# A hybrid decoder step on one core: two right sides in one product, two heads in one bank, and steps emitted a little after they are ready

## The chip, the core and the metric

The kernel runs on one core of one Trainium2 chip. The metric is the device time of one execution in microseconds; an execution is also profiled, and the profile gives the times of single instructions. Engines are called as in the profile: PE (TensorE) with PEld for its weight loads, DVE (VectorE), ACT (ScalarE), POOL (GpSimd) and SP (SyncE, which issues most transfers).

## The reference

One layer of a decoder for 1024 prompt tokens and 8 sequences of 8 new tokens, 1024 features:

```
h = rms_norm(x) * (1 + scale) + shift          # scale, shift, gate from silu(c) @ w_ada
P = h @ w_in                                   # RWKV columns, pooling columns, gate columns
for each token t, head by head (8 heads of 64):    # the RWKV-7 state
    sa = S @ (-kk_t)
    S = S * w_t + outer(sa, kk_t * a_t) + outer(v_t, k_t)
    y_t = S @ r_t
merged = sigmoid(g_A) * (A @ w_br_rwkv) + sigmoid(g_B) * (B @ w_br_pool)
x = x + gate * (merged @ w_out)
x = x + gate2 * (square(relu(h2 @ w_ff1)) @ w_ff2)
```

A is y after a group norm, a bonus and an output gate; B is a causal multi-scale mean of the pooling columns. The prompt starts from a zero state, each sequence from its own. All is float32; outputs are the rows of x after a last norm and the new states.

## The kernel before, in words

Features lie on partitions, the 1088 tokens along the free axis. A large product is done in three passes of rounded high and low parts (mm3): a row of 128 output features takes three chunks of 362 or 364 tokens. These large products are the backlog of the first stage: 34 blocks of w_in, then 8 blocks of w_br for the pooling branch, 36 or 72 products each. The output stage follows with 8 blocks of w_br for the RWKV branch (or_job), whose first 27 products read the rows of the first three head pairs and whose 28th is the first to read the rows of the fourth; then come w_out and the two layers of the channel mixer.

Beside the backlog run the head pairs f = 0 to 3 (two heads of 64 features each on the two halves of the partitions, HB). For each, front makes decay, keys and values, scores and unit make the products of a chunk of 64 tokens in groups of eight chunks (u = 0, 1) and of the 64 sequence tokens (u = 2), inverse and level make z, the inverse of a triangular matrix per chunk, affine applies z (first) and folds the result into the chunk's matrices (second), chain carries the state S through 16 chunks, sample does the sequences, and post makes the rows of A. The state chain is serial: a step's two products (ra with S into pn, S with ra into py, line 1138 and 1141) read S, and DVE makes the next S from pn (line 1139). In the trace these are wc<-S,ra, wc<-ra,S and the DVE writes of S. A product of line 358 has the helper's line, so tiles tell them apart: w<-at,z and w<-uv,z are first's two products with z (lines 1086 and 1087), w<-ab,at is second's (1099), w<-hv,ra and w<-ra,hv are the sequences' products with their states (1179 and 1194), w<-wt,kct are the head sums in the last post (1247 and 1252).

PE runs its instructions in the order in which the program emits them. That order is planned while the program is built. Pace holds a planned time; the backlog yields after each three products, and generators for chains, heads and pools yield what they wait for. Need is such a wait: at() is the planned time at which tiles are ready and PSUM banks free, and the step is emitted when the planned time has passed it. Where PE is amid large products, a ready step is held back up to `wait` ns more, so that several small steps share a trip from large to small products; where PE is at small products it is emitted at once. need has wait=500, and the chain's steps have wait=LS[f], with LS = (1200, 1200, 1200, 400). The planned times of DVE, ACT and POOL come from Clocks, which places each operation by a formula. PSUM has four banks of tag mm, two of w and two of wc.

Two orders of the heads matter below: a front for f writes bk only when the first half of the chain f-1 is done, and unit 1 starts when its second half is done.

Of the kernel before, what the change touches and what calls it, by code (L numbers as in the profile page):

```python
# [13 lines left out]
ALU = mybir.AluOpType  # L14
# [199 lines left out]
class Need:  # L214


    def __init__(self, k, aps, banks, wait):
        self.k, self.aps, self.banks, self.wait = k, aps, banks, wait

    def at(self):  # L220
        return max([self.k.clocks.ready(*self.aps)] + [self.k.clocks.free(b, self.k.pb[b], self.banks.count(b)) for b in set(self.banks)])
# [100 lines left out]
class K:  # L322
# [55 lines left out]
    def need(self, *aps, banks=("w",), wait=500):  # L378
        return Need(self, aps, banks, wait)
# [529 lines left out]
    def unit(self, f, d, u):  # L909
# [11 lines left out]
        Q = dict(ab=tl("ab", [2, 128]), ak=tl("ak", [64], 1), uv=tl("uv", [2, 64]), ra=d["qs"][u]["ra"])  # L921
        d["qs"][u] = Q
        ra, ab, ak, uv = Q["ra"], Q["ab"], Q["ak"], Q["uv"]
        if prompt:
            Q["at"] = tl("at", [64])
            strict, incl = self.kc("strict"), self.kc("incl")
        else:
            strict, incl = self.kc("strict8"), self.kc("incl8")
        for a in range(0, C, 4):
# [43 lines left out]
        if prompt:  # L973
            nc.vector.tensor_copy(Q["at"], cut(pa))
# [7 lines left out]
        if prompt:  # L982
# [6 lines left out]
            for h, os in enumerate((HB[1], HB[0])):  # L989
                nc.scalar.activation(uv[os, :, h, :], cut(ps[os, :]), AF.Copy)  # L990
# [84 lines left out]
    def affine(self, f, d):  # L1075
# [4 lines left out]
        def first(u):  # L1080
            Q = d["qs"][u]
            uv, w = Q["uv"], Q["at"]
# [24 lines left out]
        for u in range(2):  # L1107
            Q = d["qs"][u]
            yield self.need(z, Q["at"], Q["uv"], banks=("w", "w"))
# [5 lines left out]
    def chain(self, f, d):  # L1115
# [4 lines left out]
        for u in range(2):  # L1120
# [9 lines left out]
            for i in range(8):  # L1130
# [12 lines left out]
                if i < 7:  # L1143
                    yield self.need(S, banks=(), wait=LS[f])
# [12 lines left out]
    def sample(self, f, d):  # L1157
# [11 lines left out]
        px = self.ps("w")  # L1169
# [982 lines left out]
```

## Time and profile before

| | |
|---|---|
| timed runs, us | 1657.31, 1648.69, 1647.8 (median 1648.69) |
| profiled execution, us | 1655.5, span 1653.4 |
| PE busy | 1578.5 us, 95% of the span |
| DVE, ACT, POOL busy | 66%, 41%, 8% |
| granted PE clock, mean | 0.98 |
| first head's products to the output stage | 85 to 794.5 us |
| output stage to the end | 794.5 to 1653.4 us |

A row of the timeline gives start, length, engine, line, operation with output tile and inputs, shape and count, and in brackets the idle time of the engine before it and what ended it. Each float32 product leaves two records, each of the large products (float32r) one. The granted clock is a share of full speed; busy time at a granted clock of 0.66 is longer than it would be at 1.00.

### The profile page before, as it was taken

The page shows a single profiled execution, that of the slowest core. Times are in us where ns is not written, and L with a number is a line of the kernel's source. Part 1 is how long each engine was busy: PE and PEld are TensorE (multiplying, and loading weights), DVE is VectorE, ACT ScalarE, POOL GpSimd, SP SyncE. Part 2 cuts the span into 40 slices and gives each one's busy share as a digit, 9 for nine tenths or more (in the row PEclk, how much of TensorE's full clock was granted, in tenths as well). Part 3 has the DMA queues.
Part 4 walks back from the last instruction along what each step waited for, and adds up shares of the span by engine and source line. Part 5 has one row for each costly group of instructions (what it writes and reads, how often), then busy time and mean ns, then how long its engine had stood idle before and what let it go on. Part 6 is the DMA issues. An engine that isn't in the chain of part 4 may idle for free.

```text
span 1653.4 us, 35059 instructions
## 1 busy us (share of the span) xinstructions
PE 1578.5 (95%) x14363; PEld 1476.4 (89%) x14363; DVE 1091.4 (66%) x1912; ACT 674.3 (41%) x1297; POOL 137.7 (8%) x200
## 2 busy tenths in 40 slices
PE   4999999998899999999999999999999999999997
PEld 2898778887788778989999999999999999999997
DVE  5585566755659384736453578999766786666775
ACT  4455354453244444623222365222333444434651
POOL 0110011000000000000430120000000041000000
PEclk9999998999799899999999999999999999999999
DMA  9232512242223422385696456666434997665663
GB/s 345 85 106 95 181 64 86 88 162 72 70 72 102 137 87 97 107 316 187 232 340 231 154 172 204 211 218 216 174 140 145 385 355 246 200 198 158 214 200 122
DMA packets 121857, 288.28 MB, mean 174 GB/s; under 512 B 21120, under 2 KB 26752, under 8 KB 121696
## 3 DMA queue, kind: packets, MB, share of 16 engines
q1 hardware_dynamic: 113312, 264.65, 46.5%
q10 hardware_dynamic: 8240, 20.95, 3.7%
q8 instruction: 113, 1.85, 0.5%
q14 instruction: 48, 0.39, 0.1%
q0 software_dynamic: 144, 0.44, 0.1%
HBM read 208.70 MB, written 77.28 MB: 173 GB/s over the span
## 4 chain that ended last, share of the span: by engine, by line
PE 66%; DVE 8%; DMA 4%; ACT 2%; issue 2%; SPq 0%; DVEq 0%; ACTq 0%
PE mm L358 44%; PE wc L358 11%; PE w L358 11%; DVE wt L187 2%; DMA hid<-in_w_ff 1%; DVE hx L187 1%; DMA mg<-in_w_ff 1%; DVE bk L187 1%; DVE wlo L187 1%; DVE hv L187 1%; DMA hid<-in_w_ada_mlp 1%; DMA wt<-d_x 1%; ACT L187 0%; ACT wt L187 0%; PE w L389 0%
## 5 line engine op out<-in xcount | busy, mean ns | idle before, releaser
L358 PE MATMUL mm<-hx,whi 128*128 128x362 f32 (+2 forms) x2944 | 689.9, 322 | 3.9 <-ACT px L187 2.5
L358 PEld LDWEIGHTS mm<-hx,whi 128*128 128x128 f32 x2944 | 497.7, 190 | 29.4 <-issue 12.8
L358 PE MATMUL mm<-hx,wlo 128*128 128x362 f32 (+2 forms) x1472 | 463.9, 315 | 4.7 <-issue 2.4
L358 PEld LDWEIGHTS mm<-hx,wlo 128*128 128x128 f32 x1472 | 280.0, 190 | 2.8 <-DVE wlo L187 2.8
L358 PE MATMUL mm<-mg,whi 128*128 128x272 f32 (+2 forms) x1312 | 249.4, 289 | 0.1
L358 PEld LDWEIGHTS mm<-mg,whi 128*128 128x128 f32 x1312 | 205.3, 188 | 4.5 <-issue 2.5
L358 PE MATMUL mm<-mg,wlo 128*128 128x272 f32 (+2 forms) x656 | 188.5, 287 | 0.0
L358 PE MATMUL wc<-hx,whi 128*128 128x272 f32 x896 | 170.4, 287 | 0.0
L358 PEld LDWEIGHTS wc<-hx,whi 128*128 128x128 f32 x896 | 140.3, 188 | 0.0
L187 ACT ACTIVATE whi<-hid 128x512 fp32r<-128x512 f32 x128 | 80.4, 630 | 143.7 <-PE mm L358 59.4
L358 PE MATMUL wc<-hx,wlo 128*128 128x272 f32 x448 | 128.8, 287 | 0.8 <-DVE wlo L187 0.8
L358 PEld LDWEIGHTS mm<-mg,wlo 128*128 128x128 f32 x656 | 123.5, 188 | 0.0
L187 DVE TENSOR_TENSOR wlo<-hid,whi 128x512 fp32r<-128x512 f32 x128 | 87.9, 687 | 47.8 <-ACT whi L187 47.0
L187 DVE TENSOR_TENSOR wlo<-wraw,whi 128x512 fp32r<-128x512 f32 x84 | 60.8, 725 | 72.8 <-ACT whi L187 70.0
L187 ACT ACTIVATE whi<-wraw 128x512 fp32r<-128x512 f32 x100 | 62.6, 628 | 107.1 <-PE mm L358 59.3
L358 PE MATMUL w<-hx,whi 128*128 128x272 f32 (+1 forms) x480 | 97.6, 297 | 0.0
L358 PEld LDWEIGHTS wc<-hx,wlo 128*128 128x128 f32 x448 | 84.2, 188 | 1.0 <-DVE wlo L187 1.0
L187 POOL TENSOR_TENSOR hx<-hx,rs 128x64 f32<-128x64 f32 x24 | 35.2, 1465 | 569.0 <-DMA mg<-in_w_ff 379.7
L358 PEld LDWEIGHTS w<-hx,whi 128*128 128x128 f32 x480 | 77.5, 189 | 0.2 <-issue 0.2
L358 PEld LDWEIGHTS mm<-mg,hx 128*128 128x128 f32 x576 | 72.9, 188 | 5.0 <-issue 5.0
L358 PE MATMUL mm<-mg,hx 128*128 128x272 f32 (+2 forms) x576 | 75.5, 290 | 0.0
L358 PE MATMUL w<-hx,wlo 128*128 128x272 f32 (+1 forms) x240 | 71.1, 296 | 1.0 <-DVE wlo L187 1.0
(268 smaller groups left out, 2376.1 us busy)
## 6 DMA issues: line engine op xcount, KB each, us to landing
t<-d_t SPq DMA_DIRECT2D x56, 544.0 KB, 4.9
hid<-in_w_ff SPq DMA_DIRECT2D x110, 256.0 KB, 3.8
d_t<-hx SPq DMA_DIRECT2D x102, 272.0 KB, 2.2
hid<-in_w_ff SPq DMA_DIRECT2D x42, 512.0 KB, 3.9
wraw<-in_w_in SPq DMA_DIRECT2D x68, 256.0 KB, 2.9
mg<-in_w_ff SPq DMA_DIRECT2D x58, 256.0 KB, 5.4
hid<-in_w_ada_mlp SPq DMA_DIRECT2D x24, 512.0 KB, 5.9
d_th<-px SPq DMA_DIRECT2D x22, 544.0 KB, 3.1
```

Source lines behind the costliest of these rows:

```text
L187: return f(*a, **kw)
L358: return self.nc.tensor.matmul(out, lhsT, rhs, **kw)
```

## The change

The first two products with z have the same left side, z of a chunk. Before, their right sides lay in two tiles (at and the far half of uv); now at has room for both side by side, and first makes one product of 128 columns, four chunks to a bank. The strict product ak of the prompt's units shares at's second half, and the product of ak and uv is put there in one ACT operation instead of two. first empties each bank with three operations of four chunks, six in all, instead of three of eight.

In sample the two heads' products with the states are put in one bank and emitted one behind the other (before, a bank each, with a wait between), one DVE operation masks both, and the 16 products of 8 columns alternate between the heads.

In the planner, need's wait goes from 500 to 1000 and a new `spare` is added to the time at which tiles are ready (not to that of the banks): 300 ns, and 700 for the chain's steps; LS becomes (2500, 2500, 2500, 300).

```diff
@@ class Need
-    def __init__(self, k, aps, banks, wait):
-        self.k, self.aps, self.banks, self.wait = k, aps, banks, wait
+    def __init__(self, k, aps, banks, wait, spare):
+        self.k, self.aps, self.banks, self.wait, self.spare = k, aps, banks, wait, spare
     def at(self):
-        return max([self.k.clocks.ready(*self.aps)] + [self.k.clocks.free(b, self.k.pb[b], self.banks.count(b)) for b in set(self.banks)])
+        return max([self.k.clocks.ready(*self.aps) + self.spare] + [self.k.clocks.free(b, self.k.pb[b], self.banks.count(b)) for b in set(self.banks)])
-    def need(self, *aps, banks=("w",), wait=500):
+    def need(self, *aps, banks=("w",), wait=1000, spare=300):
@@ unit
         if prompt:
-            Q["at"] = tl("at", [64])
+            at = Q["at"] = tl("at", [2, 64])
+            ak = at[:, :, 1, :]
         else:
+            ak = Q["ak"] = tl("ak", [64])
-            nc.vector.tensor_copy(Q["at"], cut(pa))
+            nc.vector.tensor_copy(at[:, :, 0, :], cut(pa))
-            for h, os in enumerate((HB[1], HB[0])):
-                nc.scalar.activation(uv[os, :, h, :], cut(ps[os, :]), AF.Copy)
+            nc.scalar.activation(at[:, :, 1, :], cut(ps), AF.Copy)
@@ affine, first
-            pw, pu = self.ps("w"), self.ps("w")
+            pss = [self.ps("w") for _ in range(2)]
             for i in range(8):
-                for h, os in enumerate((HB[1], HB[0])):
-                    self.mm(pw[os, i * 64:(i + 1) * 64], z[os, 8 * u + i, :], w[os, i, :], start=True, stop=True)
-                    self.mm(pu[os, i * 64:(i + 1) * 64], z[os, 8 * u + i, :], uv[os, i, h, :], start=True, stop=True)
-            nc.scalar.activation(w, cut(pw), AF.Copy)
-            nc.vector.tensor_copy(uv[HB[1], :, 0, :], cut(pu[HB[1], :]))
-            nc.scalar.activation(uv[HB[0], :, 1, :], cut(pu[HB[0], :]), AF.Copy)
+                for os in HB[::-1]:
+                    self.mm(pss[i // 4][os, i % 4 * 128:(i % 4 + 1) * 128], z[os, 8 * u + i, :], at[os, i, :, :].rearrange("p s j -> p (s j)"),
+                            start=True, stop=True)
+            for a, ps in enumerate(pss):
+                us = slice(4 * a, 4 * a + 4)
+                pv = ps.rearrange("p (c s j) -> p c s j", s=2, j=64)
+                nc.scalar.activation(at[:, us, 0, :], pv[:, :, 0, :], AF.Copy)
+                nc.vector.tensor_copy(uv[HB[1], us, 0, :], pv[HB[1], :, 1, :])
+                nc.scalar.activation(uv[HB[0], us, 1, :], pv[HB[0], :, 1, :], AF.Copy)
@@ affine, second
-            ab, ra, w = Q["ab"], Q["ra"], Q["at"]
+            ab, ra, w = Q["ab"], Q["ra"], Q["at"][:, :, 0, :]
@@ chain
-                    yield self.need(S, banks=(), wait=LS[f])
+                    yield self.need(S, banks=(), wait=LS[f], spare=700)
@@ sample
-        px = self.ps("w")
+        px, ps = self.ps("w"), self.ps("w")
-            if h:
-                yield self.need(ra, s0)
-            ps = self.ps("w")
             self.mm(ps[os, :], ra[hs, 0, 1, :], s0[hs, :], start=True, stop=True, tile_position=(hs.start, os.start))
-            nc.vector.tensor_tensor(qv(um[os]), qv(ps[os, :]), qm[os].unsqueeze(2).to_broadcast([64, 8, 64]), op=ALU.mult)
+        nc.vector.tensor_tensor(qv(um), qv(ps), qm.unsqueeze(2).to_broadcast([P, 8, 64]), op=ALU.mult)
-            for q in range(8):
+        for q in range(8):
+            for hs in HB:
                 self.mm(py[hs, q * 8:(q + 1) * 8], s0[hs, q * 64:(q + 1) * 64], ra[hs, 0, 0, q * 8:(q + 1) * 8], start=False, stop=q == 7)
@@
-LS = (1200, 1200, 1200, 400)
+LS = (2500, 2500, 2500, 300)
```

The order on PE at three places. First, the second head pair's chain where the front of the third runs beside it, before: hx with whi or wlo are large products, hv with ab the sequences' last ones, S with ra and ra with S a chain step.

```order
L358 MATMUL wc_4452<-S_4571,ra_3143 64x64 x2
L358 MATMUL wc_4453<-ra_3143,S_4571 64x64 x2
L358 MATMUL mm_4430<-hx_211,whi_4281 128x364
L358 MATMUL mm_4430<-hx_212,whi_4281 128x364
L358 MATMUL mm_4430<-hx_211,wlo_4282 128x364
L358 MATMUL w_4617<-hv_4599,ab_3082 64x512
L358 MATMUL w_4617<-hv_4601,ab_3082 64x512
L358 MATMUL wc_4452<-S_4605,ra_3143 64x64 x2
L358 MATMUL wc_4453<-ra_3143,S_4605 64x64 x2
```

and of the change:

```order
L358 MATMUL wc_4572<-ra_3207,S_4533 64x64 x2
L358 MATMUL w_4611<-wt_4336,sw_4334 128x288
L358 MATMUL w_4614<-wt_4336,sw_4334 128x288
L358 MATMUL mm_4442<-hx_215,whi_4430 128x364
L358 MATMUL mm_4442<-hx_216,whi_4430 128x364
L358 MATMUL mm_4442<-hx_215,wlo_4431 128x364
L358 MATMUL mm_4443<-hx_215,whi_4430 128x362
L358 MATMUL mm_4443<-hx_216,whi_4430 128x362
L358 MATMUL mm_4443<-hx_215,wlo_4431 128x362
L358 MATMUL w_4642<-hv_4567,ab_3143 64x512
L358 MATMUL w_4642<-hv_4569,ab_3143 64x512
L358 MATMUL wc_4571<-S_4605,ra_3207 64x64 x2
```

Between two steps there were three large products and the sequences' two; now there are six, two of the front and the sequences' two. The next step stood 18 large products behind and now stands 33. Over a head's 15 steps, the first and the last lie 174, 87, 126 and 57 large products apart before, and 237, 237, 207 and 87 in the change, from the first head pair to the last.

Second, the last head pair's sequences, before (w_7945 and w_7955 are the two heads' products with the states):

```order
L358 MATMUL w_7941<-uv_6822,ak_6821 64x64 x2
L358 MATMUL w_7945<-hv_7900,ra_6817 64x512
L358 MATMUL wc_7772<-S_7935,ra_6494 64x64 x2
L358 MATMUL wc_7773<-ra_6494,S_7935 64x64 x2
L358 MATMUL w_7955<-hv_7900,ra_6817 64x512
...
L358 MATMUL w_8017<-ab_6820,uv_6822 64x64
L358 MATMUL w_8017<-ra_6817,hv_7900 64x8 x8
```

and of the change:

```order
L358 MATMUL w_8023<-uv_6894,ak_6895 64x64 x2
L358 MATMUL w_8024<-hv_7967,ra_6890 64x512 x2
L358 MATMUL wc_7903<-S_8017,ra_6579 64x64 x2
L358 MATMUL wc_7904<-ra_6579,S_8017 64x64 x2
...
L358 MATMUL w_8099<-ab_6893,uv_6894 64x64 x2
L358 MATMUL w_8099<-ra_6890,hv_7967 64x8 x16
```

The two heads' products now follow each other in one bank, and the 16 products of 8 columns, eight of one head and then eight of the other before, are one run in which the heads alternate.

Third, the last small product of the head pipeline (w<-wt,kct, a sum over a head in the last post), before:

```order
L358 MATMUL mm_8277<-hx_8060,whi_8202 128x362
L358 MATMUL mm_8277<-hx_8062,whi_8202 128x362
L358 MATMUL mm_8277<-hx_8060,wlo_8203 128x362
L358 MATMUL w_8285<-wt_8108,kct 128x362
L358 MATMUL mm_8278<-hx_8060,whi_8202 128x362
```

and of the change:

```order
L358 MATMUL mm_8341<-hx_7445,whi_8251 128x362
L358 MATMUL mm_8341<-hx_7447,whi_8251 128x362
L358 MATMUL mm_8341<-hx_7445,wlo_8252 128x362
L358 MATMUL w_8391<-wt_8169,kct 128x362
L358 MATMUL mm_8414<-hx_7433,whi_8329 128x364
```

Before, it stands in the third of the eight blocks for the pooling branch, 210 large products ahead of the output stage; in the change it stands ahead of the eighth, 36 large products ahead of it. The large products alone stand in one and the same order in both. PE has 158 unbroken stretches of them in the first stage before and 154 in the change.

More of the change, by code (lines that the diff above doesn't have):

```diff
@@ L376, in room @@
         return Room(self, eng, ns)
-    def need(self, *aps, banks=("w",), wait=500):
-        return Need(self, aps, banks, wait)
+    def need(self, *aps, banks=("w",), wait=1000, spare=300):
+        return Need(self, aps, banks, wait, spare)
     def tr(self, out, in_, ident):
@@ L920, in unit @@
         tl = lambda tag, shape, n=2: self.p1.tile([P, C] + shape, F32, tag=f"{tag}{C}", bufs=n if prompt else 1, name=self.nm(tag))
-        Q = dict(ab=tl("ab", [2, 128]), ak=tl("ak", [64], 1), uv=tl("uv", [2, 64]), ra=d["qs"][u]["ra"])
+        Q = dict(ab=tl("ab", [2, 128]), uv=tl("uv", [2, 64]), ra=d["qs"][u]["ra"])
         d["qs"][u] = Q
-        ra, ab, ak, uv = Q["ra"], Q["ab"], Q["ak"], Q["uv"]
+        ra, ab, uv = Q["ra"], Q["ab"], Q["uv"]
         if prompt:
-            Q["at"] = tl("at", [64])
+            at = Q["at"] = tl("at", [2, 64])
+            ak = at[:, :, 1, :]
             strict, incl = self.kc("strict"), self.kc("incl")
@@ L1108, in affine @@
             Q = d["qs"][u]
-            yield self.need(z, Q["at"], Q["uv"], banks=("w", "w"))
+            yield self.need(z, Q["at"], banks=("w", "w"))
             first(u)
```

4 lines of the change are left out of this document (2 added, 2 removed).

## The prediction

> **What bounds the kernel now.** I read the table of time stretches first, cut at 85 us (the head pipeline's first products) and at 794.5 us (the first product of the output stage). Its columns are the stretch, its length, the busy time of PE, weight loads, DVE, ACT and POOL, the granted PE clock, the DMA share and GB/s.
>
> ```profile
> 85.00:794.50 709.50, 669.73 (x7371) 594.17 (x7370) 447.70 (x811) 305.92 (x625) 43.52 (x95) 0.96 0.36 120
> 794.50:1653.40 858.90, 847.39 (x6654) 832.62 (x6652) 600.57 (x1040) 328.09 (x612) 85.86 (x69) 1.00 0.63 216
> ```
>
> Both stretches are bound by PE. The second is full at clock 1.00, and the change leaves its code alone. In the first PE is idle for 709.5 - 669.7 = 39.8 us, and it also runs slow in places. The same table for the five places with a low clock:
>
> ```profile
> 185.00:195.00 10.00, 7.58 (x217) 6.72 (x219) 1.41 (x2) 2.68 (x5) 0.63 (x2) 0.83 0.29 92
> 215.00:220.00 5.00, 5.00 (x57) 4.67 (x49) 1.40 (x4) 0.77 (x2) 0.00 (x0) 0.66 0.00 0
> 245.00:260.00 15.00, 13.28 (x97) 9.83 (x94) 12.57 (x23) 3.10 (x9) 2.54 (x2) 0.66 0.25 74
> 405.00:440.00 35.00, 28.10 (x209) 19.96 (x210) 27.31 (x45) 11.03 (x21) 1.90 (x3) 0.66 0.15 49
> 535.00:550.00 15.00, 10.31 (x143) 6.72 (x143) 7.96 (x13) 9.17 (x15) 0.00 (x0) 0.66 0.23 74
> ```
>
> Busy time by (1 - clock): 7.58 x 0.17 = 1.3, 5.00 x 0.34 = 1.7, 13.28 x 0.34 = 4.5, 28.10 x 0.34 = 9.6, 10.31 x 0.34 = 3.5, together 20.6 us. So 39.8 + 20.6 = 60.4 us of the first stretch is not work. The list of waits (who waited, for whom, us, times, longest) and the timeline say for what:
>
> ```profile
> PE wc L358 <- DVE S L187: 12.0, 8, 2.4
> PE w L358 <- ACT wt L187: 4.8, 3, 3.9
> PE w L358 <- DVE zf L187: 3.8, 1, 3.8
> 214.73 0.27 PE L358 MATMUL wc<-S,ra 64*64 64x64 f32 x2 [2.18 <-DVE S L187]
> 247.65 0.33 PE L358 MATMUL wc<-S,ra 64*64 64x64 f32 x4 [1.72 <-DVE S L187]
> 423.12 0.33 PE L358 MATMUL wc<-S,ra 64*64 64x64 f32 x4 [2.28 <-DVE S L187]
> 437.18 0.48 PE L358 MATMUL wc<-S,ra 64*64 64x64 f32 x4 [2.43 <-DVE S L187]
> ```
>
> The largest single cause is the state chain: a step's products were queued on PE before DVE had made S, and everything behind them on PE stood still. Three of the five slow places hold such a stall or follow one.
>
> **The two products in one.** Here are the two products with z of one group of eight chunks, and behind them a product that already has 128 columns (start, length, then what):
>
> ```profile
> 705.75 0.34 PE L358 MATMUL w<-at,z 64*64 64x64 f32 x4
> 705.91 0.29 PE L358 MATMUL w<-uv,z 64*64 64x64 f32 x4
> ...
> 707.80 0.60 PE L358 MATMUL mm<-hx,whi 128*128 128x362 f32 x2
> 710.98 1.96 PE L358 MATMUL w<-ab,at 64*64 64x128 f32 x32
> 712.88 0.60 PE L358 MATMUL mm<-hx,whi 128*128 128x362 f32 x2
> ```
>
> Today 64 records of 64 columns take 707.80 - 705.75 = 2.05 us, 32 ns each. The nearest row to the new product is w<-ab,at: 32 records of 128 columns in 1.90 us, 59 ns each. Half the instructions, twice the columns: the pair was limited by columns, not by its number. The gain is 0.15 us for each of 8 groups, 1.2 us; if instructions were what costs it would be half of 2.05, 8.2 us in all, and the other end is 0. I take 1.2. ACT and DVE empty the banks in halves (six operations instead of three), and the earlier copy of the at product becomes one operation instead of two; both engines have room in the first stretch (447.7 and 305.9 of 709.5 us busy) so I cost this at nothing.
>
> **The sequences' products.** Now one head, then the other:
>
> ```profile
> 727.16 0.59 PE L358 MATMUL w<-hv,ra 64*64 64x512 f32 x1
> 727.60 0.59 PE L358 MATMUL w<-hv,ra 64*64 64x512 f32 x1
> 733.61 1.09 PE L358 MATMUL w<-ra,hv 64*64 64x8 f32 x16
> 734.63 0.33 PE L358 MATMUL w<-ab,uv 128*64 128x64 f32 x2
> ```
>
> A record of 512 columns takes 0.44 us alone, 0.86 ns a column. In w<-ab,at, whose heads alternate and whose two heads write one bank, 128 columns take 59 ns, 0.46 ns a column: two run at once. So four records go from 1.76 to 0.88 us, for 4 heads 3.5 us. The small ones take 734.63 - 733.61 = 1.02 us per head, 64 ns a record; alternating records of the chain's step (below) take 46 ns. 32 records: 2.04 to 1.47, 0.57 x 4 = 2.3 us (0 if nothing overlaps, 4.1 if it halves). Together 5.8 us, between 0 and 7.6.
>
> The Trainium skill (TensorEngine Tiling (Array Packing), Gotcha 1: PSUM Pressure) speaks against this: different row tiles cannot access the same PSUM bank at once. By that rule the term is 0 and the sum below is 5.8 us smaller; w<-ab,at at 59 ns a record does not agree with it, which is why it gets only a small chance.
>
> **A trip from large to small products.** What one costs:
>
> ```profile
> 724.81 0.50 PE L358 MATMUL mm<-hx,whi 128*128 128x364 f32 x2
> 725.41 0.33 PE L358 MATMUL wc<-S,ra 64*64 64x64 f32 x4
> 725.57 0.28 PE L358 MATMUL wc<-ra,S 64*64 64x64 f32 x4
> 725.78 0.60 PE L358 MATMUL mm<-hx,whi 128*128 128x362 f32 x2
> 726.39 0.49 PE L358 MATMUL mm<-hx,whi 128*128 128x362 f32 x2
> 798.53 0.49 PE L358 MATMUL w<-hx,whi 128*128 128x362 f32 x2
> 799.02 0.49 PE L358 MATMUL mm<-hx,whi 128*128 128x364 f32 x2
> ```
>
> Three large products take 0.49 us (798.53 to 799.02), 0.165 each. Before a step they take 0.60, after it 0.61, so a trip there and back costs 0.23 us beside the step's own 0.37 (8 records, 46 ns each). The order has 158 stretches of large products before and 154 now: 4 x 0.23 = 0.9 us. Work on PE falls by 1.2 + 5.8 + 0.9 = 7.9 us.
>
> **Steps emitted later.** This is the main term. In the order the first to the last step of a head's chain lie 174, 87, 126 and 57 large products apart before, and 237, 237, 207 and 87 now. That is 1.4 to 2.7 times the time for DVE at most places; but a few steps still follow each other closely (the first place shown with the change: three large products between two steps became six). The stall of 2.43 us behind three became about 0.5 us of cover more, so it shrinks and does not vanish. I take 9 of the 12.0 us on S as gone (0 if the stalls only move, 12 at most). Of the slow clock, the places at 215 (1.7), 245 (4.5) and half of 405 (its idle is half S: 4.8) belong to S, 11.0 us; with 9/12 of the stalls goes 8.
>
> The other 39.8 - 12.0 = 27.8 us are 25 stalls elsewhere, 21 of them at a step that needs a tile or a bank. Each such step now waits 0.3 us more in the plan: at most 21 x 0.3 = 6.3, I take 6, and 2 us of the remaining 9.6 us of slow clock with it. The rest of these (3.9 us on ACT, 3.8 on DVE zf, both much longer than 0.3) is drawn anew by a new order; I leave it at its size, and give it a range of 10 us both ways.
>
> **What is late next.** Later steps push the heads back against the large products. The end of the last head before:
>
> ```profile
> 758.50 0.85 PE L358 MATMUL w<-wt,kct 128*128 128x362 f32 x2
> 768.69 0.54 DVE L187 TENSOR_TENSOR hx<-wt,hx 128x362 fp32r<-128x362 f32 x1 [0.57 <-ACT hx L187]
> ```
>
> From its last small product to its finished rows it is 769.23 - 758.50 = 10.7 us. The rows are first read by the 28th product of the output stage, which is the row at 799.02: 29.8 us to spare. In the order 210 large products stood between that small product and the output stage, now 36. With the 27 that don't need the rows, 63 x 0.165 = 10.4 us and the small product's own 0.7: 11.1 us of cover for 10.7. The spare time is used up, and I cost it at 0, with 3 us as its bad end.
>
> **The sum.** 7.9 + 9 + 8 + 6 + 2 = 32.9 us. The profiled execution took 1655.5 us (span 1653.4), 6.8 above the median of the runs shown, 1648.7. I take half of that 6.8 as stalls that the timed runs don't have, and so 32.9 - 3.4 = 29.5 off the median: **1619 us**.
>
> **The rivals.** *The stalls only move* (22%). The plan's times for DVE and ACT are off by more than 0.3 us where it hurts: 3.9 and 3.8 us. If the new order draws as many stalls as the old one, only the work goes: 1648.7 - 7.9 = 1641. For it speaks that more than half of the idle time is not on S; against it, that the four long S stalls all lie where steps stood close.
>
> *The heads outlast the large products* (6%, slower). The chains are longer by 63 + 150 + 81 + 30 = 324 large products, 53.5 us. The front of the next head waits for the first half of a chain and its second unit for the second half. If all of it landed on the heads, their last rows would come at 769.2 + 53.5 = 822.7 instead of by 799.0: 23.7 us later, 1672 us. It decides from 29.8 us of delay. Against it: the order itself moves the last small product by only 174 large products, 28.7 us, and stalls that go bring the heads forward by as much.
>
> *Nearly all stalls go* (9%). 60.4 + 7.9 = 68.3 us would give 1580; the heads' own waits keep some, say 1587. Against it: the stalls on ACT wt and DVE zf.
>
> *One bank serializes the two heads* (5%). If products of two heads that write one bank ran one after the other, the 5.8 us of the sequences' products would stay: 1619 + 6 = 1625. The 59 ns of w<-ab,at speak against it. This is what the rule of the Trainium skill named above would do here.
>
> **How the numbers follow.** My forecast has 58%, from 1600 to 1632. With its two faster companions (9% and 5%) it makes 72% for faster by over 1% (below 1632, about what a measurement of this kernel can tell from no change); stalls that only move are the 22% within 1%; the heads' delay is the 6%. The range takes the forecast, most of the moved stalls (1641 with some us more) and a part of the good case: 1595 to 1648.
>
> **What would show it.** Right: the waits of PE on S fall from 12.0 to about 3 us, idle PE between the first head and the output stage from 39.8 to about 25, the slow clock's loss from 20.6 to about 10; w<-at,z at 59 ns a record of 128 columns; a pair of w<-hv,ra in 0.9 us for four records; the heads' last rows within 3 us of the moment when the output stage reads them. Wrong: PE waiting on hx rows at the start of the output stage, or as much idle time in the first stretch with other names in it.

## The result and the profile after

The changed kernel takes 1640.3 us (median of 15 executions, 1637.8 to 1648.5); the kernel before, in 15 executions beside it, 1654.2 (1647.8 to 1657.3). The ratio is 0.9924 [0.991, 0.9937]: 13.8 us, 0.8% faster, where 1619 us and over 1% had been forecast; 1640.3 us lies inside the forecast range of 1595 to 1648, where it falls among the moved stalls. The profiled execution fell from a span of 1653.4 to 1637.1 us.

The same two stretches as in the prediction, of the changed kernel (stretch, length, busy time of PE, weight loads, DVE, ACT and POOL, granted PE clock, DMA share, GB/s):

```profile
85.00:778.90 693.90, 647.90 (x7112) 581.78 (x7111) 445.18 (x812) 311.58 (x639) 37.70 (x95) 0.98 0.36 122
778.90:1637.10 858.20, 846.60 (x6653) 832.38 (x6652) 603.49 (x1043) 328.75 (x613) 85.95 (x69) 1.00 0.63 216
```

The whole difference arises in the first stretch, which is 15.6 us shorter; the output stage has its old length. In the first stretch PE stands idle for 693.9 - 647.9 = 46.0 us, 6.2 us more than before. Its longest waits there (who waited, for whom, us, times, longest; other rows of the list are left out):

```profile
PE mm L358 <- ACT px L187: 9.3, 5, 3.5
PE w L358 <- DVE tt L187: 5.5, 1, 5.5
PE w L358 <- DVE hv L187: 5.2, 2, 5.1
PE w L358 <- DMA wt<-d_x: 4.4, 1, 4.4
PE w L358 <- ACT wt L187: 4.4, 5, 2.0
...
PE wc L358 <- DVE S L187: 3.2, 2, 1.8
PE wc L358 <- ACT y L187: 3.0, 1, 3.0
```

The state chain, first of the list before with 12.0 us, is down to 3.2. In its place stand names that were small or absent: 42.8 us are not on S, against 27.8 before. "As much idle time in the first stretch with other names in it" was one of the two signs by which the prediction was to be known as wrong. Two of the places that ran at a clock of 0.66 before, at 215 and at 245 us, now run at 1.00, and of the one from 405 to 440 there is a part left:

```profile
215.00:225.00 10.00, 10.00 (x110) 8.70 (x111) 5.01 (x11) 6.03 (x12) 0.77 (x4) 1.00 0.09 28
245.00:260.00 15.00, 13.60 (x149) 11.84 (x145) 13.07 (x22) 4.35 (x9) 1.76 (x4) 1.00 0.34 105
430.00:440.00 10.00, 9.38 (x52) 9.08 (x53) 8.25 (x15) 2.63 (x6) 1.46 (x2) 0.83 0.43 120
```

But new slow places have come, at the new stalls:

```profile
305.00:315.00 10.00, 8.13 (x28) 6.77 (x29) 8.25 (x26) 2.25 (x4) 0.00 (x0) 0.66 0.10 39
585.00:600.00 15.00, 11.29 (x51) 8.82 (x49) 13.04 (x18) 10.89 (x15) 0.32 (x1) 0.66 0.29 92
```

The products that the change rewrites, as groups of the first stage (count, busy time, mean ns), before:

```profile
L358 PE MATMUL w<-at,z 64*64 64x64 f32 x256 | 16.0, 221 | 0.0
L358 PE MATMUL w<-uv,z 64*64 64x64 f32 x256 | 15.7, 218 | 0.0
L358 PE MATMUL w<-ra,hv 64*64 64x8 f32 x128 | 10.7, 216 | 0.0
L358 PE MATMUL w<-hv,ra 64*64 64x512 f32 x16 | 8.8, 657 | 3.9 <-ACT wt L187 3.9
```

and after:

```profile
L358 PE MATMUL w<-at,z 64*64 64x128 f32 x256 | 15.7, 272 | 0.0
L358 PE MATMUL w<-ra,hv 64*64 64x8 f32 x128 | 4.4, 200 | 0.0
L358 PE MATMUL w<-hv,ra 64*64 64x512 f32 x16 | 4.1, 590 | 0.0
```

The first two of before ran interleaved, so their times lie over each other. The sequences' products fell from 19.5 to 8.5 us. Single places of the changed kernel show how:

```profile
716.22 1.96 PE L358 MATMUL w<-at,z 64*64 64x128 f32 x32
718.12 0.60 PE L358 MATMUL mm<-hx,whi 128*128 128x362 f32 x2
...
735.17 0.60 PE L358 MATMUL w<-hv,ra 64*64 64x512 f32 x2
735.60 0.60 PE L358 MATMUL w<-hv,ra 64*64 64x512 f32 x2
...
742.14 1.10 PE L358 MATMUL w<-ra,hv 64*64 64x8 f32 x32
743.17 1.15 PE L358 MATMUL wc<-uv,ab 128*64 128x64 f32 x32
```

32 records of 128 columns take 718.12 - 716.22 = 1.90 us, 59 ns each. Two records of 512 columns start together and take 0.43 us (735.17 to 735.60), where one took 0.44 before. The 32 records of 8 columns, heads alternating, take 1.03 us, 32 ns each and half of before.

**Where the time went.** I split the first stretch of each profile into PE's idle time, the slow clock's loss (busy time by one minus the granted clock, summed over stretches of 5 us), and the rest, which is the work at full clock; cut this way the work is good to some 3 us (an estimate).

| us of the first stage | before | predicted change | after | measured change |
|---|---|---|---|---|
| idle on S | 12.0 | -9 | 3.2 | -8.8 |
| idle on anything else | 27.8 | -6 | 42.8 | +15.0 |
| slow clock | 21.2 | -10 | 12.1 | -9.1 |
| work of PE | 648.6 | -7.9 | 635.7 | -12.9 |
| output stage | 858.8 | 0 | 858.2 | -0.6 |

Three of the four terms came close to the forecast or went beyond it. One has the wrong sign and misses its forecast by 21 us.

### The profile page after: what moved, and what is told of

Same layout as the page of the kernel before. It is cut to its first block, busy times and chain, and to the rows that moved or that the text cites. A ratio compares the mean times of both kernels' runs of the same rounds, so it can differ in the third digit from the quotient of the medians.

```text
span 1637.1 us, 34576 instructions
## 1 busy us (share of the span) xinstructions
PE 1555.8 (95%) x14107; PEld 1463.0 (89%) x14107; DVE 1092.3 (67%) x1916; ACT 681.1 (42%) x1313; POOL 131.9 (8%) x200
## 4 chain that ended last, share of the span: by engine, by line
PE 59%; DMA 5%; DVE 4%; ACT 2%; issue 1%; POOL 1%; SPq 0%; DVEq 0%; ACTq 0%; POOLq 0%
PE mm L358 39%; PE wc L358 12%; PE w L358 8%; DMA wt<-d_x 1%; DMA mg<-in_w_ff 1%; DMA hid<-in_w_ff 1%; DMA hx<-d_oph 1%; POOL t L187 1%; DVE hx L187 1%; DVE hv L187 1%; DMA wraw<-in_w_br 1%; DVE wlo L187 1%; DMA t<-d_th 0%; DVE bk L187 0%; DVE px L187 0%
## 5 line engine op out<-in xcount | busy, mean ns | idle before, releaser
L358 PE MATMUL mm<-hx,whi 128*128 128x362 f32 (+2 forms) x2944 | 690.7, 322 | 10.7 <-ACT px L187 9.3
L358 PEld LDWEIGHTS mm<-hx,whi 128*128 128x128 f32 x2944 | 499.0, 190 | 34.3 <-issue 12.0
L187 POOL TENSOR_TENSOR hx<-hx,rs 128x64 f32<-128x64 f32 x24 | 35.2, 1466 | 569.3 <-DMA mg<-in_w_ff 361.5
```

Of the source, the lines that this page charges most:

```text
L187: return f(*a, **kw)
L358: return self.nc.tensor.matmul(out, lhsT, rhs, **kw)
```

## The experiments

Two theories were to be told apart. *A: the new stalls have a cause of their own*, the pools' product w<-px,plw (the pooled rows px, made by DVE, times the pooling weights plw), which is queued in PE's order as soon as the plan, with its 0.3 us, believes DVE to be done. *B: the stalls are drawn anew with every order*, and this order is one draw. In the changed kernel the two long stalls at that product are

```profile
306.87 2.76 PE L358 MATMUL w<-px,plw 128*128 128x364 f32 x4 [5.05 <-DVE hv L187]
...
497.22 1.55 PE L358 MATMUL w<-px,plw 128*128 128x364 f32 x2 [5.45 <-DVE tt L187]
```

and this is DVE ahead of the first of them:

```profile
301.36 1.23 DVE L187 TENSOR_TENSOR bk<-bk,end 128x1024 f32<-128x1024 f32 x1
302.50 0.15 DVE L187 TENSOR_TENSOR zf<-d,kct 128x1 f32<-128x1 f32 x1
...
302.71 0.69 DVE L187 TENSOR_TENSOR hv<-iv,kct 128x512 f32<-128x512 f32 x1
303.31 1.03 DVE L187 STREAM_TRANSPOSE iv<-iv 128x512 f32<-128x512 f32 x1
...
304.78 1.22 DVE L187 SCALAR_TENSOR_TENSOR px<-d,px 128x1024 f32<-128x1024 f32 x1
305.91 0.74 DVE L187 SCALAR_TENSOR_TENSOR hv<-iv,kct,hv 128x512 f32<-128x512 f32 x1
306.58 0.15 DVE L187 COPY px<-zf 128x1 f32<-128x1 f32 x1
```

DVE has no gap here. The pooled rows px are finished by its copy of 306.58 to 306.73; among the pools' own steps stand those of a unit (bk) and of the inverse (hv, iv). PE stood from 301.8 to 306.87 behind a product whose input was still in this queue. The releaser that the profile names, hv, is DVE's instruction right behind that copy.

All runs, with the ratio to the kernel before on the same chip (its median there lies between 1652.9 and 1656.0, so ratios compare runs better than times); idle, slow clock and work as in the table above, "pools" the part of the idle time in front of w<-px,plw. Time and ratio are medians, the parts are those of the one execution that was profiled, which lies up to 8 us beside the median (1657.0 against 1664.6 for the kernel before with a wait of 450):

| run | time us | ratio [95%] | idle | on S | pools | slow clock | work |
|---|---|---|---|---|---|---|---|
| before | 1654.2 | 1 | 39.8 | 12.0 | 3.9 | 21.2 | 648.6 |
| after | 1640.3 | 0.9924 [0.991, 0.9937] | 46.0 | 3.2 | 11.1 | 12.1 | 635.7 |
| products only | 1658.6 | 1.003 [1.0017, 1.0044] | 52.5 | 13.2 | 19.0 | 16.4 | 639.4 |
| numbers only | 1654.2 | 1.0003 [0.9989, 1.0017] | 46.6 | 6.0 | 13.5 | 18.5 | 641.5 |
| products, chain's numbers | 1657.1 | 1.0021 [1.001, 1.0032] | 59.6 | 10.7 | 21.5 | 16.7 | 635.0 |
| products, needs' numbers | 1658.7 | 1.0024 [1.0006, 1.0042] | 51.6 | 14.0 | 13.6 | 22.2 | 637.3 |
| after, late pools | 1633.9 | 0.9869 [0.9844, 0.9894] | 38.2 | 14.8 | 2.7 | 14.8 | 632.6 |
| products only, late pools | 1646.5 | 0.9969 [0.9953, 0.9985] | 45.6 | 14.4 | 7.9 | 18.1 | 637.5 |
| after, o_ws on SP | 1643.8 | 0.9945 [0.9927, 0.9963] | 46.0 | 4.4 | 13.3 | 15.8 | 634.9 |
| after, spare 400 | 1628.1 | 0.9847 [0.9828, 0.9867] | 35.2 | 5.2 | 7.3 | 13.6 | 635.1 |
| after, spare 250 | 1629.8 | 0.9858 [0.9838, 0.9878] | 36.3 | 6.8 | 7.3 | 8.6 | 634.3 |
| after, spare 700 | 1627.9 | 0.9829 [0.981, 0.9848] | 35.2 | 4.4 | 6.7 | 10.8 | 636.3 |
| before, wait 450 | 1664.6 | 1.0057 [1.0034, 1.0081] | 43.2 | 5.5 | 6.5 | 19.8 | 649.1 |
| before, spare 100 | 1660.4 | 1.0026 [1.0009, 1.0044] | 42.3 | 8.0 | 4.4 | 18.8 | 648.5 |
| numbers only, spare 400 | 1661.5 | 1.0042 [1.0027, 1.0057] | 49.4 | 4.8 | 16.4 | 21.4 | 641.8 |
| numbers only, spare 700 | 1640.3 | 0.9909 [0.9891, 0.9926] | 42.3 | 1.7 | 16.4 | 10.9 | 640.8 |
| products only, wait 450 | 1656.8 | 1.001 [0.9998, 1.0022] | 51.1 | 13.6 | 8.5 | 20.7 | 639.1 |
| sequences' product, spare 400 | 1649.1 | 0.996 [0.9947, 0.9974] | 49.5 | 4.1 | 23.1 | 15.8 | 632.5 |
| after, pools read hx | 1634.2 | 0.9887 [0.9871, 0.9903] | 38.8 | 3.2 | 6.0 | 13.1 | 634.4 |
| after, spare 700, late pools | 1621.0 | 0.9814 [0.9793, 0.9836] | 31.8 | 4.5 | 5.2 | 5.2 | 636.1 |

### The parts by themselves

Products only is the changed kernel with the old numbers of the planner:

```diff
-    def need(self, *aps, banks=("w",), wait=1000, spare=300):
+    def need(self, *aps, banks=("w",), wait=500, spare=0):
...
-                    yield self.need(S, banks=(), wait=LS[f], spare=700)
+                    yield self.need(S, banks=(), wait=LS[f], spare=0)
...
-LS = (2500, 2500, 2500, 300)
+LS = (1200, 1200, 1200, 400)
```

> The change's products and copies with the old planner numbers: need's wait 500, no spare, LS as before. Theory A (the work term was too small, the planner's part cancels itself): PE's busy time from 85 us to the output stage falls by 10 to 13 us, ratio to before about 0.993. Theory B (the work is worth the 7.9 us of the prediction, the planner the rest): ratio 0.995, and idle PE and slow clock stay near 40 and 21 us. Theory C (the products are worth more, and the planner's numbers lose): ratio below 0.990. In all of them four records of w<-hv,ra take 0.9 us and the 32 small ones 1.0.

Numbers only is the kernel before with the planner's part of the change (the same lines the other way, and `spare` in Need).

> The kernel before with the change's planner numbers alone: wait 1000, spare 300, 700 for the chain's steps, LS (2500, 2500, 2500, 300). Theory A: PE's waits on S fall from 12 to about 3 us and other waits rise by as much or more; ratio 0.998 to 1.003. Theory B: ratio 0.997 or less. Theory C: ratio above 1.003.

The products with the chain's numbers alone leave the first of the three edits at the old values (`wait=500, spare=0`, the other two as in the change):

> The change with the chain's numbers (LS 2500, spare 700) but need's old ones for all other steps (wait 500, no spare). If the chain's numbers bring the gain on S and need's numbers bring the new waits, this is faster than the change, ratio 0.985 to 0.990, with S under 4 us and other idle time under 30. If new waits come with any new order, it is near the change, 0.990 to 0.995, with its idle time at other places.

The products with the needs' numbers alone have `wait=1000, spare=300`, and for the chain `spare=0` and the old LS:

> The change with need's new numbers (wait 1000, spare 300) but the chain's steps as before (LS 1200, no spare). If need's numbers bring the new waits: slower than the change, ratio 0.995 to 1.000, S at 8 to 12 us and other idle time at 40 or more. If new waits come with any new order: 0.990 to 0.997, S at 8 to 12 us, other idle time anywhere from 25 to 40.

Measured: 1658.6, 1654.2, 1657.1 and 1658.7 us; none is faster than before, though the work of PE is 7 to 14 us less in each. The numbers alone came within the ratio of the theory A of their expectation (the letters in these four name other theories than A and B above); the other three are slower than anything that was expected of them. What the work gained went into idle time: 52.5, 46.6, 59.6 and 51.6 us against 39.8, and above all in front of one product. The group w<-px,plw in the run of the products with the chain's numbers (busy, mean ns, then idle before it and its releasers):

```profile
L358 PE MATMUL w<-px,plw 128*128 128x364 f32 (+2 forms) x24 | 11.3, 565 | 21.5 <-issue 17.3 <-DVE px L187 3.7 <-ACT uv L187 0.5
```

against the kernel before:

```profile
L358 PE MATMUL w<-px,plw 128*128 128x364 f32 (+2 forms) x24 | 9.8, 508 | 3.9 <-issue 2.7 <-DVE px L187 0.7 <-ACT uv L187 0.5
```

One stall of 17.3 us there is more than the change gained. The profile names no releaser for it (issue), but PE goes on at 416.31, right behind DVE's last step for px, and DVE's queue has no gap in the 17 us ahead of that:

```profile
416.04 0.16 DVE L187 COPY px<-zf 128x3 f32<-128x3 f32 x1
```

Four runs with one order each cannot tell "the parts bring nothing alone" from "four bad draws"; the next runs are made for that.

### The pools' product later

```diff
-                yield self.need(z[:, c0:c0 + m], plw, zs, wait=0)
+                yield self.need(z[:, c0:c0 + m], plw, zs, wait=0, spare=5000)
```

In the changed kernel:

> The whole change, with one call altered: the need of the pools' product w<-px,plw gets a spare of 5000 in place of 300. Theory A, that the stalls which took the place of the chains' are above all the pools' own (they are emitted the moment DVE is expected to be done, with a wait of 0, and DVE is up to 5 us late): the two of 5.05 and 5.45 us go, with some 3 us of slow clock behind them, idle 46 to 36 us, and the time is 10 to 14 us under the changed kernel's 1640, 1626 to 1630. Theory B, that each new order draws stalls of its own and the changed one's are no worse than another's: the two go, others come, idle stays at 42 to 52 us and the time within 5 us of 1640.

In the products only:

> The products of the change under the old numbers of the planner (the first experiment), and the same spare of 5000 on the pools' product. Theory A: the first experiment's pools' stalls (10.65, 2.08, 2.98 and 2.07 us, 17.8 together) go, and the time falls from 1658.6 to 1638 to 1644, below the kernel before. Theory B: other stalls come, idle stays at 45 to 58 us, the time within 6 us of 1658.6.

Measured 1633.9 (0.9869 against 0.9924 for the change) and 1646.5 (0.9969 against 1.003): 9 and 10 us of the kernel before's time (0.0055 and 0.0061 of 1654). The pools' stalls went as A said, from 11.1 to 2.7 and from 19.0 to 7.9. But in the first run S stalls came back (3.2 to 14.8 us), and its output stage took 864.7 us in place of 858.2, with PE waiting 2.05 and 1.59 us on the transfer hid<-in_w_ada_mlp near 820 us (its profiled execution, 1637.4 us, was the slowest of its six). Both times lie between what A and B expected: something takes a part of the place. The kernel before was not run with a later pools' product.

### One stall taken out of an unchanged order

```diff
-        nc.scalar.dma_start(self.io["o_ws"][f], s0)
+        nc.sync.dma_start(self.io["o_ws"][f], s0)
```

> The whole change with the DMA o_ws<-hv issued on SP's queue in place of ACT's; PE's, DVE's and POOL's order stay the same, row for row, and on ACT only these four issues go. If a stall that is taken away from an unchanged order is gained in full, PE's wait of 3.54 us on ACT px near 430 us goes and the time falls by 3 to 5 us, to 1635 to 1637. If the large products wait for something else there anyway (the next wait takes it), the time stays within 1.5 us of 1640.

Measured 1643.8 us, 0.9945 [0.9927, 0.9963]: no gain, near the second case. PE's order is the changed kernel's, row for row. The two stalls of the changed kernel near that place were

```profile
430.62 0.60 PE L358 MATMUL mm<-hx,whi 128*128 128x362 f32 x2 [3.54 <-ACT px L187]
441.07 1.49 PE L358 MATMUL w<-px,plw 128*128 128x364 f32 x4 [0.62 <-DVE px L187]
```

and in this run they are

```profile
431.46 0.33 PE L358 MATMUL wc<-S,ra 64*64 64x64 f32 x4 [1.41 <-DVE S L187]
441.35 2.79 PE L358 MATMUL w<-px,plw 128*128 128x364 f32 x4 [2.78 <-DVE px L187]
```

3.54 + 0.62 = 4.16 us there, 1.41 + 2.78 = 4.19 us here. In both the pools' product starts 0.05 us behind the end of DVE's copy to px (441.02 and 441.30): with ACT's late step gone, DVE is the limit. That both start at 441 us is in part chance, since this profile runs 2 us late before the place (its product of 306.87 starts at 308.85). Of the 3.54 us some 1.7 were thus gained up to here, and lost again further on: the first stretch ends at 781.7 us in place of 778.9.

### Redraws of the order

The changed kernel with another spare, 400, 250 and 700 in place of 300:

```diff
-    def need(self, *aps, banks=("w",), wait=1000, spare=300):
+    def need(self, *aps, banks=("w",), wait=1000, spare=400):
```

> The whole change with the spare of a need at 400 in place of 300, a change with no aim: some 570 lines of PE's 7550 rows move. Theory A, that each stall has a cause that the planner's numbers set: idle 44 to 48 us as in the changed kernel, the time within 2 us of 1640. Theory B, that the stalls are drawn anew with any shift of the order: idle moves by 4 to 10 us to either side and the time by 4 to 12 us, above rather than below, since the numbers shown are one draw among many.

> The whole change with the spare of a need at 250 in place of 300. Theory B, the stalls are drawn anew with each order and follow no trend in the spare: idle anywhere in 35 to 47 us, the time 1628 to 1644, whichever side of the 1640 of 300. Theory C, that a larger spare is what took the 11 us off in the run with 400 (each step that much surer to find its input): idle 46 to 48 us, the time 1640 to 1643.

> The whole change with the spare of a need at 700, that of the chains. Theory B: idle anywhere in 35 to 47 us, the time 1628 to 1644. Theory C, a trend: idle 30 us or less, the time 1615 to 1625, and the waits that are left are those of needs without a spare's help (the pools', a DMA).

Measured 1628.1, 1629.8 and 1627.9 us. The run with 400 moves 216 of PE's 7550 rows (the 570 lines of the expectation count both sides and their marks) and gains 12 us on the changed kernel. Idle is 35 to 36 us in all three against 46.0, and there is no trend from 250 to 700: A, as it was put for these runs, and C fall. B has the size of the shift, though it looked for a rise. The kernel with 300 is the odd one among its neighbours. The first stretch of the run with 400, and then two of its waits:

```profile
85.00:769.00 684.00, 648.75 (x7115) 582.49 (x7115) 444.78 (x815) 308.97 (x639) 37.86 (x95) 0.98 0.37 124
```

```profile
PE wc L358 <- DVE S L187: 5.2, 3, 3.3
PE mm L358 <- ACT px L187: 2.7, 2, 1.5
```

Of the changed kernel's 46.0 us, the stall of 5.45 at 497 us is not there, and the large products wait 2.7 us on ACT px in place of 9.3. But not every stall is drawn anew. The first one at the pools, 5.05 us at 306.87, stands in this order too, and at 5.05 us in the one with 250:

```profile
308.44 2.76 PE L358 MATMUL w<-px,plw 128*128 128x364 f32 x4 [5.06 <-DVE hv L187]
```

With 700 it is 1.59 us, and with the late pools it is gone (in the numbers alone with 700, below, it is 5.05 again). It has a cause of its own, as A says.

The kernel before, redrawn by a wait of 450 in place of 500, and by a spare of 100 for every need:

```diff
-    def need(self, *aps, banks=("w",), wait=500):
+    def need(self, *aps, banks=("w",), wait=450):
```

> The kernel before with the wait of a need at 450 in place of 500, with no aim; 920 of the printed lines of PE's order differ. If the idle of 39.8 us of the order before was a lucky draw that any new order loses (and the rise that I did not predict comes from that), idle is 44 to 54 us and the time 5 to 14 us over 1654. If the rise belongs to what the change adds, idle stays at 37 to 43 us and the time within 3 us of 1654.

> The kernel before with a spare of 100 ns on every need that has none, a second redraw with little aim; 400 lines differ. As for the wait of 450: 44 to 54 us of idle and 5 to 14 us over 1654 if the order before was a lucky draw; 37 to 43 us and within 3 us of 1654 if not; a fall below 1648 would say that a small spare by itself helps.

Measured 1664.6 (1.0057) and 1660.4 (1.0026) us: 4 to 9 us above the kernel before, with 42 to 43 us of idle time. The times are what was expected if the order before was a lucky draw, the idle time is below that; both profiles are of executions near the fast end (1657.0 and 1655.6 us), so where the 4 to 9 us lie is not shown. So the order before is somewhat better than its neighbours and the changed one is worse than its own. The mean ratio of the three orders of before is 1.0028 (1, 1.0057 and 1.0026), of the four of the change 0.9865: by these seven orders the change is worth some 27 us (an estimate, 0.0163 of 1654), and the pair that was compared showed 13.8 of it.

### More draws of the parts

The numbers without the products, with a spare of 400 and of 700:

> The products of before with the new numbers of the planner, and 400 for 300 in a need's spare. If the numbers bring their part by themselves (S stalls and slow clock, 17 us of my sum) and the second experiment's 1654 was a poor draw: 1632 to 1642, idle 34 to 40 us. If the numbers need the new products to bring anything: 1650 to 1658, idle 43 to 50 us.

> The same with 700 for 300. As before: 1632 to 1642 if the numbers bring their part by themselves, 1650 to 1658 if not; and if the two draws differ by 8 us or more, the order by itself is worth as much as the numbers.

The products without the numbers, with a wait of 450:

> The products of the change under the old numbers, with a wait of 450 in place of 500. PE's own work is 9 to 13 us below the kernel before. If the products bring that much and the first experiment's 1658.6 was a poor draw (10.65 us at one pools' product): 1644 to 1650. If what they free always goes into stalls under the old numbers: 1654 to 1664, idle over 48 us.

The whole with a spare of 400, but `first` and the tiles ab, ak, at and uv as before, so that only the sequences' product is new:

> The whole change with 400 for 300, but the two right sides of the solve in products of their own, as before: of the new products only the sequences' are left. By my sum the merged product is worth 1.2 us of the work and the sequences' 5.8, so work is 1 to 2 us above that of the run with 400 (635.1) and the time, if the order draws alike, 1628 to 1633. If the merged product carries the 5 us of work that I had not foreseen: work 640 to 643 and 1633 to 1638.

Measured 1661.5 and 1640.3 us for the numbers: 21 us apart, with nothing but the spare between them, one above both cases and one in the better of them. The products under the old numbers stay at 1656.8, as the second case had it: the pools' stall is down from 19.0 to 8.5 us, but 13.6 are still on S. Alone, then, the numbers bring anything from -7 to 15 us. The products are best judged against the run that has the same numbers and the old products. Under the old numbers they lose 5 us at a wait of 500 (1.003 against 1) and gain 8 at a wait of 450 (1.001 against 1.0057). Beside the new numbers they gain 13, 32 and 13 us at a spare of 300, 400 and 700 (0.9924, 0.9847 and 0.9829 against 1.0003, 1.0042 and 0.9909). They take 4 to 10 us off the work in all five pairs; how much of the time follows is a matter of the order. With the sequences' product alone under the new numbers 1649.1, outside both ranges, and this is its group at the pools:

```profile
L358 PE MATMUL w<-px,plw 128*128 128x364 f32 (+2 forms) x24 | 12.5, 647 | 23.1 <-DVE px L187 12.6 <-DVE tt L187 5.9 <-DVE hv L187 4.6
```

Its work, 632.5 us, is not above the 635.1 of the whole with the same spare: the merged right sides take no visible work off PE, and the sequences' product carries 9 us (641.8 to 632.5, both with a spare of 400). Its order draws 14 us more idle time than the whole's, with the pools' wait 16 us longer, and its output stage is 6 us longer (865.2 against 858.8); why is not shown.

### Is the pools' wait what the changed kernel lost?

The changed kernel with the pools' product reading rows that are there from the start:

```diff
-                self.mm(ps[:, :m], plw, z[:, c0:c0 + m], start=True, stop=True)
+                self.mm(ps[:, :m], plw, self.hh[0][:, c0:c0 + m].bitcast(F32), start=True, stop=True)
```

and the same for zs. This leaves the pools' part out of the result.

> The whole change, but the pools' products read rows of hx in place of the pooled values that DVE makes (so the pools' part of the result is left out), emitted at the same rows of PE's order: PE's rows are the changed kernel's, with that operand alone exchanged; some steps of DVE and ACT change places. The wait of 11.1 us in front of them is then gone. If that wait is what the changed kernel lost: idle 46 to 33 to 36 us, the time 1640 to 1626 to 1630. If the next wait takes most of it: idle 40 to 46 us, the time 1635 to 1641.

Measured 1634.2 us, 0.9887 [0.9871, 0.9903], 6 us under the change. The group at the pools is

```profile
L358 PE MATMUL w<-hx,plw 128*128 128x364 f32 (+3 forms) x32 | 9.9, 432 | 6.0 <-DVE px L187 6.0
```

so 5.1 of the 11.1 us went (the last piece of a product now waits for a step of DVE that empties a bank, and that stands late in the same queue), and idle fell by 7.2. What was taken away was gained nearly in full; it was half of what I had expected to take. So A and B are both true in part: the wait at the pools has its own cause and costs what it lasts, and how long it lasts differs from order to order.

### The best order

The whole with a spare of 700, and 1500 for the pools' product:

```diff
-                yield self.need(z[:, c0:c0 + m], plw, zs, wait=0)
+                yield self.need(z[:, c0:c0 + m], plw, zs, wait=0, spare=1500)
```

> The whole change with a need's spare at 700 and the pools' product's at 1500. The wait in front of it, 6.7 us in the run with 700, falls to 2 to 5 us. If nothing takes its place: 1623 to 1627, the fastest of all. If the order draws another stall: 1628 to 1638.

Measured 1621.0 us, 0.9814 [0.9793, 0.9836]: 32 us under the kernel before on the same chip (1653.4), 2 us below the best that was expected. It is the lowest time and ratio of all, though its interval overlaps that of a spare of 700 alone (0.9829 [0.981, 0.9848]), so that the 1500 brought anything is not shown. Its first stretch, and then its waits of the large products and on S:

```profile
85.00:758.10 673.10, 641.38 (x7108) 575.48 (x7107) 445.19 (x815) 306.32 (x636) 35.94 (x95) 0.99 0.37 126
```

```profile
PE mm L358 <- ACT px L187: 5.6, 8, 1.4
PE wc L358 <- DVE S L187: 4.5, 3, 1.8
```

No wait in front of the pools is over 1.6 us now, none of the large products' over 1.4, and the slow clock costs 5.2 us in place of 21.2.

## Why the prediction was wrong, step by step

**The work** (7.9 us): right in kind and too small, 12.9. The merged right sides are at the 59 ns a record that w<-ab,at gave, and bring next to nothing, as costed (1.2). The sequences' products were the mis-sized term: hv,ra 8.8 to 4.1 us (4.7, I had 3.5), ra,hv 10.7 to 4.4 (6.3, I had 2.3 by the chain step's 46 ns; the end at which they halve, 4.1, was the right one, and at single places 64 ns a record became 32). A part of the groups' fall is slow clock that went. The numbers by themselves take 7 us off the work (648.6 to 641.5, 641.8 and 640.8); 7 stretches fewer with a spare of 300, by 0.23 us, explain 1.6 of that; the rest stays open.

**One bank serializes the two heads** (the rival by the rule of the Trainium skill, TensorEngine Tiling (Array Packing), Gotcha 1: PSUM Pressure): no. Two heads that write one bank by turns took half the time of one head after the other, in both products.

**The stalls on S and their slow clock** (9 + 8 us): right for this order, 8.8 us, and with the 2 us put down to other places 9.1 us of slow clock. One reading was short: of the 6.9 us idle from 405 to 440, the two S stalls shown are 4.7, two thirds and not half; by the prediction's own rule the 8 should have been some 9.5. The mechanism, steps queued before DVE had made S, holds on average: the 13 runs with the chain's new numbers have 5.7 us on S in the mean, the 7 without them 11.5. But it is not the whole of it. Two of the 13 have 10.7 and 14.8, and the kernel before falls from 12.0 to 5.5 by a wait of 450 that leaves the chain's numbers alone. So a part of the 8.8 is luck of the order.

**"Each such step now waits 0.3 us more in the plan ... I take 6"** and **"the rest ... is drawn anew by a new order; I leave it at its size"**: this is the step that failed. The other stalls rose by 15.0 us where they were to fall by 6. The 0.3 us are a margin against a plan that is off by up to 5 us: PE waited 5.05 and 5.45 us at the pools' product, whose need has a wait of 0 and whose input DVE makes in program order, behind steps of two other sequences of work. And leaving a redraw at its size took the order before for an average one. Its 27.8 us not on S were a low draw: 37.7 and 34.3 in its two redraws. Over the runs the idle time not on S goes from 23 to 49 us, and the pools' part of it from 2.7 to 23.1. The 10 us both ways that I gave it were too few for this order: 21 us lie between the 21.8 that I took and its 42.8. In the three neighbours it is 30.0, 29.5 and 30.8, 8 to 9 us above what I took; there too it did not fall.

**The base** (3.4 us off): wrong. The three runs shown had a median of 1648.7, fifteen have 1654.2; the profiled execution of 1655.5 was a usual one. From 1654.2 the same gain of 29.5 us gives 1624.7, which is 1 to 6 us below what the ratios of the changed kernel's three neighbours give (1625.9 to 1630.7). That they come so near is luck in part: in the mean their work fell by some 5 us more than forecast, their slow clock by as much as forecast, their stalls on S by some 2.5 less, and their other stalls rose by 2 where they were to fall by 6. So 5.5 of the 21.3 us by which I missed come from three runs' median and 15.8 from the gain, 13.8 us in place of 29.5; of these the order with 300 accounts for some 10 to 15, by its neighbours' gains of 23.5 to 28.3.

**The rivals.** *The stalls only move* names the time, 1641, and half of the mechanism: S stalls and slow clock did go, but others took their place in this order. That its time is met to 1 us is luck: its base was 5.5 us too low and its work 5.0 too small, and the two cancel. I had given it 22%, on the ground that the long S stalls stood where steps stood close; that ground was sound and said nothing of the others. *The heads outlast the large products* did not happen, and narrowly: the last rows of hx are finished at

```profile
782.17 0.54 DVE L187 TENSOR_TENSOR hx<-wt,hx 128x362 fp32r<-128x362 f32 x1 [0.57 <-ACT hx L187]
```

782.71 us, and the output stage, which starts at 778.9, reaches them 27 products of 0.165 us later, at 783.4. The cover of 11.1 us for 10.7 held with 0.7 to spare, as forecast. *Nearly all stalls go* (1587) did not happen in any order: the best one, 1621.0, still has 31.8 us of idle time and 5.2 of slow clock.

## What to carry to other kernels

When a planner orders an in-order engine, a change of its numbers draws many of the small stalls anew: here orders of the same parts lay up to 21 us apart, nearly as much as the change was worth, so size such a change by several neighbouring settings on either side, not by one pair. A margin has to be as wide as the plan's error at the step it protects, and a step with little margin whose input comes out of a busy engine's queue is the next stall; look for those first. A stall taken away is gained only if what the engine reaches next is ready: in one case the next waits were together just as long (4.19 us for 4.16).

## What was not expected of the hardware

Products of 8 columns cost 64 ns a record when one head follows the other and 32 when the two heads alternate, though a record has so few columns. And a stall of 1.79 us left the granted clock at 1.00 in the stretch behind it, while two stalls of 1.98 and 1.73 us, 4 us apart, stand in 15 us at 0.66 (585 to 600, shown above). Of the changed kernel:

```profile
588.67 0.33 PE L358 MATMUL w<-x,z 64*64 64x64 f32 x4 [1.98 <-ACT wt L187]
593.06 2.55 PE L358 MATMUL w<-wt,sw 64*128 64x512 f32 x4 [1.73 <-ACT wt L187]
...
617.92 0.33 PE L358 MATMUL wc<-S,ra 64*64 64x64 f32 x4 [1.79 <-DVE S L187]
```

```profile
620.00:630.00 10.00, 10.00 (x91) 9.27 (x89) 4.05 (x8) 2.36 (x8) 0.00 (x0) 1.00 0.31 108
```

Nor does the length of one stall alone decide whether the clock falls. Behind a stall of 1.40 us on S near 249 us the clock stayed at 1.00 in the changed kernel's profile (245 to 260, shown above) and fell in that of the run with o_ws on SP, where PE has the same order and the same stall:

```profile
245.00:260.00 15.00, 13.60 (x150) 11.64 (x148) 13.38 (x21) 3.43 (x6) 1.77 (x4) 0.89 0.32 114
```

No run here was made to find what decides it.
